# Both parts of a split operand as one moving operand of 512 columns, into two halves of a PSUM bank

## The chip, the core and the metric

The kernel runs on one core of a Trainium2 chip. Time is device time in microseconds from the first to the last instruction of one execution; smaller is better. Runs of the kernel before gave 2663.76, 2665.52 and 2670.75 us, median 2665.52 us.

## The reference

A trunk of two layers on 256 tokens of 2048 channels, all in float32: layer 0 mixes with an RWKV-7 time mix, layer 1 with a causal convolution module, and each is followed by a gated MLP (ConvGLU). Cut to what matters here:

```
F = 5504
h = modulate(rms_norm(x, g), shift, scale)            # shift, scale, gate from c: c_act @ ada_w[i]
# layer 0
r, k, v = einsum('nbtc,ncd->nbtd', x_rkv, w_rkv)      # three 2048 x 2048 linears
y = wkv7_scan(r, decay, k, v, -kk, kk * a)            # a recurrence over the 256 tokens, per head
out = ((group_norm(y) + bonus) * g) @ w_o
# layer 1
u = glu(h @ w_pw1 + b_pw1); u = causal_depthwise_conv(u, w_dw, b_dw)
out = silu(layer_norm(u)) @ w_pw2 + b_pw2
# after each
x = x + gate * out
g, val = split(h @ w_up)                              # 2048 x 11008
x = x + gate2 * ((silu(conv3(g)) * val) @ w_down)     # 5504 x 2048
```

## The kernel before

Activations lie with channels on the 128 partitions and the 256 tokens along the free axis (`T = 256`), so a linear of 2048 inputs is 16 output tiles, each a sum over 16 input tiles. Products are made in a cheap one-pass float32 form (fp32r), and to keep precision every operand is split in two: `hi` is the rounded value and `lo` the rest. Of weights, ScalarE makes `hi` (L231) and VectorE, or for some tiles GpSimd, makes `lo` (L232) in `split_w`, from a 1 MB tile `raw` that a DMA brought; `hi` and `lo` have three buffers each. Of activations, a tile `x` (`slot(F32R)`, 2 parts of 260 columns) holds part 0 (rounded) and part 1 (rest).

`mm_pair` adds one input tile's product to a PSUM accumulator with three matmuls: hi·part 0 (L237), hi·part 1 (L238), lo·part 0 (L239). Each loads its 128x128 weights anew, so `hi` is loaded twice. The linears that feed `w_up` and `w_pw1` call it with 258 columns (two columns carry the adaLN shift); all others with 256. Of the calls with 256 columns, 1376 are in the down projections (`w_dn`: 2 layers x 16 output tiles x 43 input tiles), 96 in the last six tiles of k, 256 in r (`r_tile`), 128 in half of v (`v_gen`), 40 in the first half of five `w_o` tiles during the scan (`wo_gen`), 216 in the rest of `w_o`, 208 in `w_pw2`: 2320 together. `k_outer` holds the first three `w_pw2` tiles (48 more triples) and takes its operands one at a time.

In the order of time the stages are: the first ten tiles of k beside the token mix; the last six of k; r with decay, a, and the scan's operands; the other half of v in plain fp32 (`linear_native`, L300) while VectorE inverts 32x32 blocks (`inv_step`, two interleaved chains, one for each half X[0], X[1] of a tile `raw`); the scan, in which TensorE's order is written out by hand (a heap of generators with due times); `w_o`; the ConvGLU of layer 0 in three parts of 15, 14 and 14 hidden tiles, each an up stage and a down stage; the convolution; `w_pw2`; the ConvGLU of layer 1; the final norm. The adaLN products c·ada_w ("gates", `ada`, L208) are background work: a 1 MB tile `raw`, two multiply-and-sum pieces on VectorE. They run beside the stages up to and with `w_pw2`, and a few beside the first up stage of layer 1. Outside hand-ordered places a scheduler sets the order of each engine's instructions when the program is built; each engine then runs its own in that order.

A finished accumulator is read once: by a copy on ScalarE (k, v), by a multiplication on VectorE (r, L459), by a bias on ScalarE (`w_pw2`, L1119), or by one multiply-add on VectorE into the residual (`stt`, L159: `w_o` L893, `wo_gen` L835, `w_dn` L943). The accumulators take turns over the eight PSUM banks.

Of the kernel before, what the change touches and what calls it, by code (L numbers as in the profile page):

```python
# [18 lines left out]
P = 128  # L19
T = 256  # L20
# [91 lines left out]
def trunk_kernel(ctx: ExitStack, tc: tile.TileContext, a, out):  # L112
# [42 lines left out]
    def vmul(o, x, y):  # L155
        nc.vector.tensor_tensor(out=o, in0=x, in1=y, op=ALU.mult)  # L156
# [6 lines left out]

    # ---- constants, parameters
    cst = cp.tile([P, NCC], F32, name="cst")
# [56 lines left out]

    # ---- linear layers
    def split_w(r, k0, k1, step=1024, eng=None):
# [10 lines left out]
    def mm_pair(acc, hi, lo, j, x, first, last, n=T):  # L235
        c = slice(j * P, (j + 1) * P)
        nc.tensor.matmul(acc[:, :n], lhsT=hi[:, c], rhs=x[:, 0, :n], start=first, stop=False)  # L237
        nc.tensor.matmul(acc[:, :n], lhsT=hi[:, c], rhs=x[:, 1, :n], start=False, stop=False)  # L238
        nc.tensor.matmul(acc[:, :n], lhsT=lo[:, c], rhs=x[:, 0, :n], start=False, stop=last)  # L239
# [24 lines left out]
    class k_outer:  # L264
        """some outputs together, the operands fed one at a time; the weights split ahead, two operands' at once"""

# [20 lines left out]
        def feed(self, o):  # L287
            k = self.n
            self.n += 1
            hi, lo = self.sp[k // 2]  # L290
            for w, q in ((hi, 0), (lo, 0), (hi, 1)):
                for j, acc in enumerate(self.accs):
                    c = slice((2 * j + k % 2) * P, (2 * j + k % 2 + 1) * P)
                    nc.tensor.matmul(acc[:, :T], lhsT=w[:, c], rhs=o[:, q, :T], start=k == 0 and w is hi and q == 0, stop=k == KT - 1 and q == 1)

    def linear_native(r, hs32, tag=None):
# [4 lines left out]
        return acc  # L301

    def split_x(src, o):
        nc.scalar.copy(o[:, 0, :T], src)
        vsub(o[:, 1, :T], src, o[:, 0, :T])

    # ---- rms norm
    def sq_acc(st, x):
# [15 lines left out]

    # ================= layer 0: time mix =================
    hs = [slot() for _ in range(KT // 2)]
# [30 lines left out]
    def ada_s(f):  # L357
        lw = slot().rearrange("p a t -> p (a t)")[:, :448]
        nc.sync.dma_start(out=lw, in_=a["lw1"][f])
        # scale and shift of tile f  # L360
        pa = ps("y")
        for q in range(2):
            r = raw_tile()
            nc.sync.dma_start(out=r, in_=a["ada_s"][f, q])
            for k in range(8):
                g, kk = k % 4, 8 * q + k
                nc.tensor.matmul(pa[32 * g:32 * g + 32, :T], lhsT=cc[:, kk, :], rhs=r[:, k * T:(k + 1) * T],  # L367
                                 start=kk < 4, stop=kk >= 12, skip_group_check=True)
        rk = load_w(a["w_k"][f])
        sb = t1()  # L370
        nc.scalar.copy(sb, pa[:, :T])
        for j in range(2):
            nc.tensor.matmul(pa[:, 256 + j:257 + j], lhsT=sb[:, j * P:(j + 1) * P], rhs=K("e4"), start=True, stop=True, skip_group_check=True)
        for j in range(2):
            piece = 1 - j
            vadd(mod(0, piece, f), pa[:, 256 + j:257 + j], pc("ada_b", piece * KT + f))
        stt(geff[0][:, f:f + 1], mod(0, 1, f), 1.0, pc("gam_mix", f), ALU.add, ALU.mult)
        ahead[f] = (lw, rk)
# [57 lines left out]

    # ---- k, decay, a; A, B, K of the scan; N
    for f in range(KM, KT):
        acc = linear(a["w_rkv"][1, f], xk, ("mm", "y")[f % 2])
        kt.append(t1())  # L440
        nc.scalar.copy(kt[f], acc[:, :T])
        bg(BG_K)
# [13 lines left out]
    def r_tile(f):  # L456
        r_load(f)
        acc = linears(None, xr, ("c", "y")[f % 2], T, None, [rw.pop(f)])[0]
        vmul(pv(f)[:, :, 1:L + 1], ch(acc[:, :T]), pv(f)[:, :, 1:L + 1])  # L459
        nc.sync.dma_start(out=dAR[f, :, :, 1, :], in_=pv(f)[:, :, 1:L + 1])  # L460
# [104 lines left out]

    # ---- inverse of the 32-blocks, all heads and chunks on partitions
    X = raw_tile()
# [65 lines left out]

    # ---- v, scan, group norm, bonus, gate
    def small(tag, w, bufs):
# [7 lines left out]
    def v_gen(f):  # L643
        acc = ps("mm")
        r = load_w(a["w_rkv"][2, f])
        yield 0
        for k0 in range(0, KT, 8):
            hi, lo = split_w(r, k0, k0 + 8, 512, VE[0])
            for k in range(k0, k0 + 8):
                mm_pair(acc, hi, lo, k - k0, xv[k], k == 0, k == KT - 1)  # L650
                yield VS
        vt[f] = t1()
        nc.scalar.copy(vt[f], acc[:, :T])

# [17 lines left out]
    def prep_gen(f):  # L672
# [7 lines left out]
        yield 0  # L680
        # products of A, R with B, K, and B, K by tokens
        for c in range(NC_):
# [12 lines left out]
            yield PU  # L695
        # off-diagonal block of the inverse
        py = ps("g")
# [5 lines left out]
        for h in range(2):  # L703
            r1 = slice(h * L + 32, h * L + 64)
            nc.scalar.copy(ysb[r1].rearrange("p c t -> p (c t)"), py[r1, :P])
        # bonus
        rk = t1()
# [6 lines left out]
        yield PU  # L714
        # centred V by tokens, in the other half of the partitions
        pvt = ps("g")
# [107 lines left out]

    # half of the output projection and residual, while the scan goes on
    def wo_gen(m):
        x_load(m)
        r = load_w(a["w_o"][m][:, :C // 2])
        yield 0
        acc = ps("mm")  # L830
        hi, lo = split_w(r, 0, KT // 2, 512, VE[0])
        for k in range(KT // 2):
            mm_pair(acc, hi, lo, k, yo[k], k == 0, k == KT // 2 - 1)
            yield VS
        stt(xview(m), acc[:, :T], mod(0, 2, m), xview(m))  # L835

# [24 lines left out]
    with tc.manual_schedule(engines={mybir.EngineType.PE}):  # L861
        while heap:
# [4 lines left out]
            if d is not None:  # L867
                at(t + d, g)
    # ---- output projection and residual
    # gain * x, with the shift in the last columns: the products of the two are rstd-free  # L870
    def operand(l, which, f):
# [16 lines left out]
    for f in range(KT):  # L888
        x_load(f)
        if f >= max(NG, NWO):  # L890
            ada(0, 2, f)
        acc = waccs[f] if f < 3 else w_o(f)
        stt(xview(f), acc[:, :T], mod(0, 2, f), xview(f))  # L893
        ops.append(operand(0, 1, f))
        sq_acc(st, xview(f))
# [5 lines left out]

    # ---- ConvGLU
    def ffn(l, st, ops, nops):
# [14 lines left out]
        for f0, f1 in PARTS:  # L918
# [22 lines left out]
            for f in range(KT):  # L941
                acc = linear(a["w_dn"][l, f][:, f0 * P:f1 * P], hid, None, T, half(f, DNP))
                stt(xview(f), acc[:, :T], mod(l, 5, f), xview(f))  # L943
                if f1 == FT:
# [13 lines left out]

    # ================= layer 1: conformer convolution =================
    ops = nops  # L960
# [23 lines left out]

    # n of the taps on the tensor engine, m on GpSimd, the others on the vector engine in two chains
    def tap(f, d):
# [127 lines left out]
    for f in range(KT):  # L1114
# [3 lines left out]
        t = t1()  # L1118
        act(t, acc[:, :T], bias=pc("b_pw2", f))  # L1119
        stt(xview(f), t, mod(1, 2, f), xview(f))  # L1120
# [4 lines left out]

    # ---- final norm
    rstd = rstd_of(st)
# [108 lines left out]
```

## Time and profile before

| | |
|---|---|
| three runs | 2663.76, 2665.52, 2670.75 us; median 2665.52 |
| profiled execution, span | 2670.5 us; its own time is not given apart from the span |
| mean granted TensorE clock | 0.977 of full |
| TensorE matmul / weight load busy | 2520.7 us (94%) / 2404.8 us (90%) |
| VectorE / ScalarE / GpSimd busy | 2003.9 us (75%) / 1357.1 us (51%) / 464.0 us (17%) |
| HBM | 614.30 MB read, 235 GB/s over the span |

A matmul's end in the profile is modelled (it is pipelined), so "busy" says that TensorE had work, not how fast it ran; the distance from one matmul's start to the next one's says that. It is read from a stretch without gaps as length divided by count.

### The profile page before, as it was taken

To read this page: it belongs to the slowest core of one execution; us is meant where nothing else is said; L and a number is where in the kernel's file an instruction comes from. 1 tells how busy PE (TensorE), PEld (TensorE's weight loads), DVE (VectorE), ACT (ScalarE), POOL (GpSimd) and SP (SyncE) were. 2 spreads that over 40 slices of the span, in tenths; PEclk is the share of its full clock that TensorE was granted. 3 is DMA by queue.
4 is the path that set the end of the run, shared out by engine and by line. 5 is a ranking of instruction groups with operands and counts; after the bars stand their busy time and mean duration, and the time that the engine had idled before them with its cause. 6 is when DMAs were issued, how large, how long until landed. Compare 5 with 4: busy or idle time off the path is not lost.

```text
span 2670.5 us, 52899 instructions
## 1 busy us (share of the span) xinstructions
PE 2520.7 (94%) x21250; PEld 2404.8 (90%) x21250; DVE 2003.9 (75%) x3635; ACT 1357.1 (51%) x2650; POOL 464.0 (17%) x452
## 2 busy tenths in 40 slices
PE   6899996999999999999999999978899999999998
PEld 3678885877799999999999999967899999999997
DVE  4567767768688888887878979979988656656665
ACT  4565622556555543553455555554555445534553
POOL 0000015544000012001100248954200000000000
PEclk9999997989999999999999999989999999999999
DMA  8887766677277778777978844436777655555553
GB/s 312 316 312 268 211 207 209 230 218 240 78 284 278 283 285 331 292 281 290 336 263 296 305 161 164 168 127 243 286 275 273 220 188 188 170 190 190 178 175 126
DMA packets 154805, 630.84 MB, mean 236 GB/s; under 512 B 60480, under 2 KB 72256, under 8 KB 95936
## 3 DMA queue, kind: packets, MB, share of 16 engines
q1 hardware_dynamic: 153824, 624.85, 65.9%
q8 instruction: 166, 2.72, 0.4%
q0 software_dynamic: 736, 2.62, 0.3%
q14 instruction: 79, 0.65, 0.1%
HBM read 614.30 MB, written 13.11 MB: 235 GB/s over the span
## 4 chain that ended last, share of the span: by engine, by line
PE 76%; DVE 10%; DMA 7%; ACT 3%; issue 2%; POOL 1%; SPq 0%; DVEq 0%; POOLq 0%; ACTq 0%
PE ps L237 22%; PE ps L239 22%; PE ps L238 21%; DMA raw<-ada 4%; DVE raw L208 3%; DVE s L159 2%; DVE lo L232 1%; PE ps L367 1%; PE ps L300 1%; DMA raw<-ada_s 1%; POOL lo L232 1%; DVE s L156 1%; PE ps L687 1%; ACT hi L231 1%; PE ps L398 1%
## 5 line engine op out<-in xcount | busy, mean ns | idle before, releaser
L237 PE MATMUL ps<-s,hi 128*128 128x258 f32 (+1 forms) x5584 | 1594.8, 286 | 7.5 <-ACT hi L231 6.4
L239 PE MATMUL ps<-s,lo 128*128 128x258 f32 (+1 forms) x5584 | 1581.6, 284 | 20.8 <-DVE lo L232 18.9
L238 PE MATMUL ps<-s,hi 128*128 128x258 f32 (+1 forms) x5584 | 1579.8, 283 | 0.6 <-DVE s L153 0.6
L231 ACT CAST hi<-raw 128x1024 fp32r<-128x1024 f32 (+6 forms) x873 | 769.7, 897 | 881.8 <-PE ps L238 606.1
L239 PEld LDWEIGHTS ps<-s,lo 128*128 128x128 f32 x5584 | 1063.7, 191 | 29.4 <-DVE lo L232 22.8
L237 PEld LDWEIGHTS ps<-s,hi 128*128 128x128 f32 x5584 | 1060.2, 190 | 16.8 <-ACT hi L231 8.6
L238 PEld LDWEIGHTS ps<-s,hi 128*128 128x128 f32 x5584 | 1063.4, 190 | 4.5 <-issue 3.0
L232 DVE TENSOR_TENSOR lo<-raw,hi 128x1024 fp32r<-128x1024 f32 (+4 forms) x639 | 746.0, 1171 | 303.5 <-ACT hi L231 301.8
L232 POOL TENSOR_TENSOR lo<-raw,hi 128x512 fp32r<-128x512 f32 x234 | 335.2, 1458 | 957.5 <-ACT hi L231 623.4
L208 DVE CUSTOM_DVE_ANT_0 raw<-raw,cb,par 128x1024 f32<-128x1024 f32 x156 | 213.2, 1367 | 76.0 <-DMA raw<-ada 71.3
L208 DVE CUSTOM_DVE_ANT_0 raw<-raw,cb,md 128x1024 f32<-128x1024 f32 x156 | 214.9, 1378 | 0.9
L159 DVE SCALAR_TENSOR_TENSOR s<-ps,par,s 128x239 f32<-128x239 f32 (+26 forms) x420 | 166.0, 456 | 1.8 <-ACT s L162 1.2
L1135 POOL TENSOR_TENSOR s<-s,t 128x256 f32<-128x256 f32 x6 | 4.1, 727 | 751.4 <-DVE t L322 751.4
L156 DVE TENSOR_TENSOR t<-ps,t 128x256 f32<-128x256 f32 x188 | 79.2, 422 | 47.5 <-PE ps L239 43.8
L159 DVE SCALAR_TENSOR_TENSOR s<-ps,md,s 128x256 f32<-128x256 f32 x117 | 55.9, 480 | 41.8 <-PE ps L239 41.7
L159 DVE SCALAR_TENSOR_TENSOR t<-t,par,t 128x255 f32<-128x255 f32 (+1 forms) x172 | 82.6, 480 | 1.9 <-ACT t L162 0.6
L156 DVE TENSOR_TENSOR s<-ps,cst 64x64 f32<-64x64 f32 (+2 forms) x208 | 48.1, 253 | 37.7 <-ACT n L689 27.0
L162 ACT ACTIVATE t<-t,par 128x256 f32<-128x256 f32 x118 | 68.1, 587 | 5.6 <-DVE t L156 2.5
L162 ACT ACTIVATE t<-t 128x256 f32<-128x256 f32 x102 | 42.5, 417 | 37.9 <-DVE t L159 24.1
L687 PE MATMUL ps<-s,s 128*128 128x128 f32 x256 | 46.6, 308 | 11.6 <-ACT s L694 10.6
L300 PE MATMUL ps<-s,raw 128*128 128x256 f32 x256 | 56.0, 380 | 0.0
L300 PEld LDWEIGHTS ps<-s,raw 128*128 128x128 f32 x256 | 48.4, 190 | 6.9 <-issue 0.3
(199 smaller groups left out, 2167.2 us busy)
## 6 DMA issues: line engine op xcount, KB each, us to landing
raw<-w_up SPq DMA_DIRECT2D x172, 1024.0 KB, 4.9
raw<-ada SPq DMA_DIRECT2D x156, 1024.0 KB, 6.7
raw<-w_dn SPq DMA_DIRECT2D x64, 896.0 KB, 4.7
raw<-w_pw SPq DMA_DIRECT2D x48, 1024.0 KB, 4.9
raw<-w_rkv SPq DMA_DIRECT2D x38, 1024.0 KB, 6.0
raw<-ada_s SPq DMA_DIRECT2D x32, 1024.0 KB, 6.4
raw<-w_dn SPq DMA_DIRECT2D x32, 960.0 KB, 4.9
raw<-w_o SPq DMA_DIRECT2D x11, 1024.0 KB, 4.9
```

The lines of the kernel that those rows point to most:

```text
L156: nc.vector.tensor_tensor(out=o, in0=x, in1=y, op=ALU.mult)
L159: nc.vector.scalar_tensor_tensor(out=o, in0=x, scalar=s, in1=y, op0=op0, op1=op1)
L162: nc.scalar.activation(out=o, in_=i, func=func, bias=bias, scale=scale)
L208: nc.vector.tensor_tensor_reduce(out=r[q], in0=r[q], in1=cb[:, q * w:(q + 1) * w], scale=1.0, scalar=mod(l, piece, f) if q else pc("ada_b" ...
L231: nc.scalar.copy(hi[:, s], v[:, s])
L232: (eng or nc.vector).tensor_tensor(out=lo[:, s], in0=v[:, s], in1=hi[:, s], op=ALU.subtract)
L237: nc.tensor.matmul(acc[:, :n], lhsT=hi[:, c], rhs=x[:, 0, :n], start=first, stop=False)
L238: nc.tensor.matmul(acc[:, :n], lhsT=hi[:, c], rhs=x[:, 1, :n], start=False, stop=False)
L239: nc.tensor.matmul(acc[:, :n], lhsT=lo[:, c], rhs=x[:, 0, :n], start=False, stop=last)
L300: nc.tensor.matmul(acc[:, :T], lhsT=r[:, k * P:(k + 1) * P], rhs=hs32[k], start=k == 0, stop=k == n - 1)
L367: nc.tensor.matmul(pa[32 * g:32 * g + 32, :T], lhsT=cc[:, kk, :], rhs=r[:, k * T:(k + 1) * T], start=kk < 4, stop=kk >= 12, skip_group_che ...
L687: nc.tensor.matmul(pg[:, h * P:(h + 1) * P], lhsT=bkc, rhs=ari[h][:, c].rearrange("p j t -> p (j t)"), start=True, stop=True, skip_group_c ...
```

## The change

Where the operand has 256 columns, hi·part 0 and hi·part 1 become one matmul: both parts are one moving operand of 2 x 256 columns, and the result goes into the two halves of the bank (first half hi·part 0, second half hi·part 1). lo·part 0 is added to the second half. Each of the 2368 triples (2320 and the 48 of `k_outer`) becomes two matmuls with two weight loads, with as many columns in all (512 + 256). The sum of the halves is made when the accumulator is read: `both` copies one half on ScalarE and adds the other on VectorE; `both_res` makes two multiply-adds into the residual where there was one. r's product moves from VectorE to GpSimd behind such a sum. The linears of 258 columns stay as they are.

```diff
     def mm_pair(acc, hi, lo, j, x, first, last, n=T):
         c = slice(j * P, (j + 1) * P)
+        if n == T:
+
+            nc.tensor.matmul(acc.rearrange("p (a t) -> p a t", a=2), lhsT=hi[:, c], rhs=x[:, :, :T], start=first, stop=False, skip_group_check=True)
+            nc.tensor.matmul(acc[:, T:], lhsT=lo[:, c], rhs=x[:, 0, :T], start=False, stop=last, skip_group_check=True)
+            return
         nc.tensor.matmul(acc[:, :n], lhsT=hi[:, c], rhs=x[:, 0, :n], start=first, stop=False)
...
-            for w, q in ((hi, 0), (lo, 0), (hi, 1)):
-                for j, acc in enumerate(self.accs):
-                    c = slice((2 * j + k % 2) * P, (2 * j + k % 2 + 1) * P)
-                    nc.tensor.matmul(acc[:, :T], lhsT=w[:, c], rhs=o[:, q, :T], start=k == 0 and w is hi and q == 0, stop=k == KT - 1 and q == 1)
+            for j, acc in enumerate(self.accs):
+                mm_pair(acc, hi, lo, 2 * j + k % 2, o, k == 0, k == KT - 1)
...
+    def both(o, acc):
+        nc.scalar.copy(o, acc[:, T:])
+        vadd(o, acc[:, :T], o)
+
+    def both_res(x, acc, s):
+        stt(x, acc[:, :T], s, x)
+        stt(x, acc[:, T:], s, x)
...
-        nc.scalar.copy(kt[f], acc[:, :T])
+        both(kt[f], acc)
...
-        vmul(pv(f)[:, :, 1:L + 1], ch(acc[:, :T]), pv(f)[:, :, 1:L + 1])
+        rt = t1()
+        both(rt, acc)
+        nc.gpsimd.tensor_tensor(out=pv(f)[:, :, 1:L + 1], in0=ch(rt), in1=pv(f)[:, :, 1:L + 1], op=ALU.mult)
...
-        nc.scalar.copy(vt[f], acc[:, :T])
+        both(vt[f], acc)
...
-        stt(xview(m), acc[:, :T], mod(0, 2, m), xview(m))
+        both_res(xview(m), acc, mod(0, 2, m))
...
-                stt(xview(f), acc[:, :T], mod(l, 5, f), xview(f))
+                both_res(xview(f), acc, mod(l, 5, f))
...
-        act(t, acc[:, :T], bias=pc("b_pw2", f))
+        act(t, acc[:, T:], bias=pc("b_pw2", f))
+        vadd(t, acc[:, :T], t)
```

In the built program VectorE gets 163 instructions (117 `stt` from PSUM and 46 additions from PSUM) and loses 16 (r's products), ScalarE gets 16 copies, GpSimd 16 products.

TensorE, last down stage of layer 1, before (`s` are the activations' tiles, `ps` the accumulator):

```order
L237 MATMUL ps_30605<-s_30145,hi_30634 128x256
L238 MATMUL ps_30605<-s_30145,hi_30634 128x256
L239 MATMUL ps_30605<-s_30145,lo_30635 128x256
L237 MATMUL ps_30662<-s_28377,hi_30663 128x256
L238 MATMUL ps_30662<-s_28377,hi_30663 128x256
L239 MATMUL ps_30662<-s_28377,lo_30664 128x256
```

and in the changed kernel, where the lines of `mm_pair` are L239 and L240:

```order
L239 MATMUL ps_28404<-s_27092,hi_28405 128x512
L240 MATMUL ps_28404<-s_27092,lo_28406 128x256
L239 MATMUL ps_28404<-s_27228,hi_28405 128x512
L240 MATMUL ps_28404<-s_27228,lo_28406 128x256
L239 MATMUL ps_28404<-s_27364,hi_28405 128x512
L240 MATMUL ps_28404<-s_27364,lo_28406 128x256
```

Three rows for each input tile have become two, the first of them with 512 columns.

VectorE, first down stage of layer 0, before (`L232` makes a weight's `lo`, `L208` is a gate, and the row with `ps` and `md` adds a finished accumulator to the residual):

```order
L159 SCALAR_TENSOR_TENSOR s_8326<-ps_11510,md_72,s_8326 128x256
L232 TENSOR_TENSOR lo_11637<-raw_11633,hi_11636 128x1024
L232 TENSOR_TENSOR lo_11665<-raw_11633,hi_11664 128x896
L208 ISA raw_11749,md_73<-raw_11749,cb,par 128x1024
L208 ISA md_73 128x1
L159 SCALAR_TENSOR_TENSOR s_8326<-ps_11572,md_72,s_8326 128x256
L232 TENSOR_TENSOR lo_11694<-raw_11690,hi_11693 128x1024
```

and in the changed kernel:

```order
L232 TENSOR_TENSOR lo_11082<-raw_11058,hi_11081 128x896
L208 ISA raw_11101,md_73<-raw_11101,cb,md_73 128x1024
L208 ISA md_73 128x1
L159 SCALAR_TENSOR_TENSOR s_8039<-ps_11010,md_72,s_8039 128x256
L232 TENSOR_TENSOR lo_11109<-raw_11105,hi_11108 128x1024
L159 SCALAR_TENSOR_TENSOR s_8039<-ps_11010,md_72,s_8039 128x256
L159 SCALAR_TENSOR_TENSOR s_8147<-ps_11060,md_72,s_8147 128x256 x2
```

Each accumulator now takes two additions, in VectorE's own order between the `lo` pieces that TensorE needs next.

VectorE at the end of the inverse, before; the rows with `raw_3963` are its steps (`s_3967` belongs to the second chain), `L208` is a gate, and the last row is the inverse's last step:

```order
L627 MEMSET raw_3963 128x32
L150 TENSOR_TENSOR raw_3963<-raw_3963,s_3967 128x28x3
L208 ISA raw_4367,md_72<-raw_4367,cb,par 128x1024
L208 ISA md_72 128x1
L156 TENSOR_TENSOR s_3967<-raw_3963 128x58
L208 ISA raw_4367,md_72<-raw_4367,cb,md_72 128x1024
L208 ISA md_72 128x1
L150 TENSOR_TENSOR raw_3963<-raw_3963,s_3967 128x29x2
L156 TENSOR_TENSOR s_3967<-raw_3963 128x30
L208 ISA raw_4512,md_72<-raw_4512,cb,par 128x1024
L208 ISA md_72 128x1
L150 TENSOR_TENSOR raw_3963<-raw_3963,s_3967 128x30
```

and in the changed kernel, a stretch that begins 48 rows ahead of the inverse's last step (`s_3668` is the first chain's scratch, `s_3669` the second's; `ps_4073` with `cst` are masked products of the scan's first tile):

```order
L208 ISA raw_4199,md_72<-raw_4199,cb,par 128x1024
L208 ISA md_72 128x1
L156 TENSOR_TENSOR s_3668<-raw_3665 128x84
L641 MEMSET raw_3665 128x32
L150 TENSOR_TENSOR raw_3665<-raw_3665,s_3669 128x21x10
L156 TENSOR_TENSOR s_3674<-ps_4073,cst 64x64
L156 TENSOR_TENSOR s_3675<-ps_4073,cst 64x64
L208 ISA raw_4199,md_72<-raw_4199,cb,md_72 128x1024
L208 ISA md_72 128x1
L150 TENSOR_TENSOR raw_3665<-raw_3665,s_3668 128x28x3
L645 COPY s_4040<-raw_3665 128x512
L156 TENSOR_TENSOR s_3669<-raw_3665 128x198
```

Before, three gate pieces and no masked product stand ahead of the inverse's last step (counted from the inverse's beginning); now six gate pieces and twelve masked products (four chunks of three) do.

## Rows read from the trace of the kernel before

**Rows 1.** The page's first and fourth parts: busy time of each engine, and the chain.
```profile
PE 2520.7 (94%) x21250; PEld 2404.8 (90%) x21250; DVE 2003.9 (75%) x3635; ACT 1357.1 (51%) x2650; POOL 464.0 (17%) x452
...
PE 76%; DVE 10%; DMA 7%; ACT 3%; issue 2%; POOL 1%; SPq 0%; DVEq 0%; POOLq 0%; ACTq 0%
```

**Rows 2.** Windows by stage: stretch, length; busy (x) PE, PEld, DVE, ACT, POOL; clock, DMA, GB/s.
```profile
184.00:225.00 41.00, 40.94 (x330) 39.97 (x330) 31.02 (x39) 23.04 (x42) 0.14 (x2) 1.00 0.88 326
225.00:357.00 132.00, 130.32 (x1082) 112.53 (x1082) 100.37 (x184) 79.51 (x126) 12.54 (x35) 1.00 0.72 218
357.00:437.00 80.00, 66.09 (x352) 58.56 (x352) 54.64 (x173) 15.77 (x44) 27.86 (x23) 0.93 0.61 198
437.00:720.00 283.00, 255.70 (x2802) 215.15 (x2802) 199.36 (x508) 162.27 (x564) 113.46 (x114) 0.92 0.62 203
720.00:799.00 79.00, 77.15 (x623) 75.48 (x624) 63.43 (x111) 42.31 (x78) 0.00 (x0) 0.98 0.67 243
971.00:1058.00 87.00, 85.80 (x722) 85.39 (x721) 74.17 (x97) 33.43 (x43) 25.82 (x16) 1.00 0.83 314
1218.00:1304.00 86.00, 82.01 (x678) 81.39 (x676) 68.25 (x97) 31.49 (x43) 20.39 (x16) 0.98 0.85 318
1465.00:1549.00 84.00, 80.95 (x676) 79.78 (x675) 76.87 (x131) 44.46 (x92) 21.74 (x18) 1.00 0.83 299
1822.00:1911.00 89.00, 73.65 (x560) 71.37 (x560) 89.00 (x131) 41.32 (x89) 39.20 (x24) 0.94 0.71 270
2089.00:2174.00 85.00, 85.00 (x722) 85.00 (x721) 45.43 (x51) 32.50 (x36) 0.00 (x0) 1.00 0.56 191
2174.00:2336.00 162.00, 162.00 (x1345) 162.00 (x1344) 103.20 (x139) 83.87 (x139) 0.00 (x0) 1.00 0.52 180
2336.00:2415.00 79.00, 79.00 (x671) 79.00 (x670) 42.83 (x50) 30.47 (x34) 0.00 (x0) 1.00 0.57 192
2577.00:2657.00 80.00, 79.56 (x676) 79.35 (x674) 46.10 (x63) 36.55 (x53) 0.00 (x0) 1.00 0.42 139
```

**Rows 3.** Groups by line and shape, TensorE: one of three lines of `mm_pair`, 256 columns.
```profile
L239 PE MATMUL ps<-s,lo 128*128 128x256 f32 x2320 | 658.7, 285 | 20.0 <-DVE lo L232 18.1 <-POOL lo L232 1.9
```

**Rows 4.** Groups of the page: the plain fp32 matmuls (L300) and their weight loads.
```profile
L300 PE MATMUL ps<-s,raw 128*128 128x256 f32 x256 | 56.0, 380 | 0.0
...
L300 PEld LDWEIGHTS ps<-s,raw 128*128 128x128 f32 x256 | 48.4, 190 | 6.9 <-issue 0.3
```

**Rows 5.** Timeline of TensorE: start, length of a merged run, count.
```profile
365.65 6.64 PE L300 MATMUL ps<-s,raw 128*128 128x256 f32 x30
```

**Rows 6.** Timeline of weight loads: eight loads that feed matmuls of one column.
```profile
1645.34 0.98 PEld L982 LDWEIGHTS ps<-cst,s 128*128 128x128 f32 x8
```

**Rows 7.** Groups of the page, VectorE: pieces that read PSUM, and one gate.
```profile
L156 DVE TENSOR_TENSOR t<-ps,t 128x256 f32<-128x256 f32 x188 | 79.2, 422 | 47.5 <-PE ps L239 43.8
...
L159 DVE SCALAR_TENSOR_TENSOR s<-ps,md,s 128x256 f32<-128x256 f32 x117 | 55.9, 480 | 41.8 <-PE ps L239 41.7
...
L208 DVE CUSTOM_DVE_ANT_0 raw<-raw,cb,par 128x1024 f32<-128x1024 f32 x156 | 213.2, 1367 | 76.0 <-DMA raw<-ada 71.3
```

**Rows 8.** Waits of VectorE, first down stage of layer 0.
```profile
DVE raw L208 <- DMA raw<-ada: 9.2, 6, 3.2
```

**Rows 9.** Groups on VectorE in the `w_pw2` stage: the longest of one shape.
```profile
L159 DVE SCALAR_TENSOR_TENSOR s<-t,md,s 128x256 f32<-128x256 f32 x13 | 11.3, 870 | 0.0
```

**Rows 10.** Timeline of VectorE: first and last step of the inverse, masked products.
```profile
380.01 0.19 DVE L156 TENSOR_TENSOR s<-raw 128x30 f32<-128x30 f32 x1 [15.65 <-DMA raw<-dN]
...
428.41 0.20 DVE L150 TENSOR_TENSOR raw<-raw,s 128x30 f32<-128x30 f32 x1
...
428.65 0.66 DVE L156 TENSOR_TENSOR s<-ps,cst 64x64 f32<-64x64 f32 x3
```

**Rows 11.** Waits of TensorE in the scan stage.
```profile
PE ps L702 <- DMA tn<-dTn: 4.5, 1, 4.5
...
PE ps L730 <- DMA s<-dT: 4.2, 1, 4.2
```

More of the change, by code (lines that the diff above doesn't have):

```diff
@@ L892, in trunk_kernel @@
         acc = waccs[f] if f < 3 else w_o(f)
-        stt(xview(f), acc[:, :T], mod(0, 2, f), xview(f))
+        both_res(xview(f), acc, mod(0, 2, f))
         ops.append(operand(0, 1, f))
```

## Prediction

> **What bounds the kernel now.** I read the page first: TensorE has work for 94% of the span and makes up 76% of the chain that ended last, VectorE 10% of it [rows 1]. That average hides stages with different limits, so I cut the span into stages [rows 2] and compared TensorE's length per matmul with VectorE's busy time. In the two down stages of layer 1 without a gap, 85.00 us hold 722 matmuls and 79.00 us hold 671: 117.7 ns from start to start, at a granted clock of 1.00 (2.4 GHz), with VectorE busy little over half. There nothing but the matmul's own beat counts. In layer 0 the down stages carry the gates as well: VectorE is busy 74.17 of 87, 68.25 of 86 and 76.87 of 84 us, and DMA moves 299 to 318 GB/s. The `w_pw2` stage is the other extreme: VectorE is busy for all of its 89.00 us, TensorE for 73.65. The scan and what leads to it wait on chains of short pieces.
>
> **What a triple costs, and a pair.** Of the matmuls with 256 columns there are 2320 on each of three lines [rows 3]; three of them take 3 x 117.7 = 353.1 ns. The trace has no fp32r matmul of 512 columns, so its beat x is bounded. From above: columns alone set the beat, and 512 take twice what 256 take, x = 235.4; the gain g = 353.1 - (x + 117.7) is then nothing. From below: at 2.4 GHz and a column a cycle 512 columns need 213.3 ns, so 256 need 106.7, and 11.0 ns of each 117.7 are something else. What that is decides. Eight weight loads that feed matmuls of one column, where no stream of columns can be the limit, take 0.98 us [rows 6]; less 0.19 for the last one's own length, the mean of such a load [rows 4], that is 0.79 / 7 = 113 ns a load. A load is therefore longer than 106.7 ns of columns, and a triple looks like three loads in a row, each not quite hidden. The plain fp32 matmul has a longer beat, (6.64 - 0.38) / 29 = 215.9 ns [rows 4, 5], and its load costs nothing visible. I take x = 215.9 as the nearest row: a long matmul covers the load behind it, g = 353.1 - 215.9 - 117.7 = 19.5 ns. At most the short matmul too falls to the 113 ns of the load, g = 24.
>
> The Trainium skill (TensorE: Matmul & The Clock Gate, "Back-to-back issue gap") gives the gap as N / 2.4 + 2.5 ns, 109.2 for 256 columns and 215.8 for 512. By it alone a triple is 327.5 and a pair 325.0, and the change is worth 2.5 ns a triple. The trace disagrees for 256 columns (117.7) and agrees for the longer plain matmul. The same page ("LDWEIGHTS (loading the stationary operand)") gives a load of 128 columns 107 ns, which with the 113 ns above speaks for the load as what is left.
>
> **The change, part by part** (gain with g = 19.5, against the profiled span):
> - Layer 1's down stages: 688 triples, all on the path. VectorE gets 16 more pieces of 480 ns [rows 7], 7.7 us, beside 45.43 of 85 and 42.83 of 79 us [rows 2]: hidden. -13.4 us.
> - `w_o`: 216 triples are 4.2 us. VectorE goes from 63.43 of 79 us to 71.1 of 75 and will be late now and then. I take -3.
> - k: 96 triples, 1.9 us, but the stage moves 326 GB/s, the most of any [rows 2]. -1.5. r: 256 triples, 5.0 us, TensorE at 130.32 of 132 us. VectorE trades a product for an addition, GpSimd's 16 products lie beside 12.54 busy of 132 us. -4.
> - v and `wo_gen` in the scan: 168 triples, 3.3 us. TensorE has 27 us without work there, so part of the gain becomes wait. Half: -1.5.
> - Layer 0's down stages: again 688 triples or 13.4 us, but VectorE gets 7.7 us a stage. Busy plus new is 81.9, 76.0 and 84.6 of 87, 86 and 84; the third is already over. Its idle 37.7 us in the three stages (87 - 74.17 and so on) is largely waits for a gate's DMA, 9.2 us in the first [rows 8], which shrink if VectorE comes later. If the cover holds the sum is -13.4, if the waits stay as they are it is +23. Queued behind a late addition are the `lo` pieces that TensorE waits for (18.1 us over the kernel, [rows 3]). I take -2.
> - `w_pw2`: 16 more additions from PSUM on the engine that has no idle time: 16 x 0.422 [rows 7] = +6.7 us. TensorE's 4.1 us for 208 triples buy nothing. Bounds: nothing if they fill a hole, 13.9 if they were stretched as the SBUF form of this stage, 870 ns [rows 9], where the same operation from PSUM has 480 over all stages. `k_outer` now waits for an operand's rest before its first matmul; its 0.9 us go there: 0.
> - The end of the inverse. In the new order three more gate pieces (1.37 us each, [rows 7]) and four groups of masked products (0.66 us, [rows 10]) stand ahead of the inverse's last step, which releases the copy that the scan waits for: TensorE stood 4.5 and 4.2 us for it [rows 11]. 3 x 1.37 + 4 x 0.66 = 6.7 us; the gates are then done and don't come later. The products also wait for TensorE. Bounds 0 and 10; I take +4.
>
> Sum: -13.4 - 3 - 1.5 - 4 - 1.5 - 2 + 6.7 + 4 = -14.7 us. The profiled span is 2670.5 us, 5.0 over the median of the three runs and within them, so I subtract from the median: 2665.5 - 14.7 = **2651 us**.
>
> **Rivals.**
> *Columns set the beat.* x = 235.4, g = 0: a matmul's reading of its operand takes 0.46 ns a column whatever the load does. For it: 258 columns take 162.00 / 1345 = 120.4 ns [rows 2], 2.7 ns more for two columns, which a load that is the limit would not show. Against it: the plain matmul's 215.9, and the bare load's 113. All TensorE terms vanish, the costs stay: +6.7, +4, and in layer 0's down stages about a quarter of the 23 us that VectorE gets, +6: 2682 us, slower. It decides from g below about 9 ns on: the TensorE terms are worth 1.2 us per ns (23.4 / 19.5), so 9 ns just pay the 10.7 us of `w_pw2` and the inverse. The Trainium skill's gap formula gives 2.5 ns, which is this case with 3 us less.
> *A fixed price per matmul.* The 11.0 ns belong to each matmul, whatever its length: x = 224.3, g = 11.1. 13.3 us of gain against 10.7 of cost and about 1 in layer 0: 2664 us, no change.
> *VectorE takes TensorE's place in layer 0.* g is as forecast, but the gates' waits do not shrink and every added piece delays a `lo`: the three stages cost 23 us instead of gaining 2. For it: 84.6 of 84 us in the third. Against it: gates are background work and 37.7 us idle are there. It decides once more than some 15 of the 23 us are not covered: -14.7 + 2 + 23 = +10, 2676 us; with half of them covered 2664.
>
> **Chances and numbers.** Forecast 0.50 (its own range 2640 to 2660: g from 15 to 24 and the bounds of `w_pw2` and the inverse), fixed price 0.18, columns 0.17, VectorE 0.15. Three runs of this kernel spread by 0.26%, so 0.3%, 8 us, is about what tells a change from none. Faster: 0.46 of the forecast and 0.04 of the others; slower: 0.14 of the columns and 0.06 of VectorE; the rest, 0.30, no change. The range 2640 to 2680 reaches from the best of the forecast to the columns' case and leaves out about a tenth on either side.
>
> **What would show it.** In layer 1's down stages a pair should take 334 ns from one 512-column start to the next, and a stage of 240 pairs about 80 us in place of 85; 353 ns would be the columns, 342 the fixed price. `w_pw2` should be some 7 us longer with VectorE busy throughout. In layer 0 the down stages should stay near 86 us with VectorE above 90%. From the start of the inverse's first step to its last, VectorE should need some 7 us more than the 48.6 from 380.01 to 428.61 before [rows 10]. The prediction fails if x is not near 216, or if the new order starts the scan much later than I allow.

## The result, and the profile after

The changed kernel is slower. Its runs gave 2687.72 to 2698.05 us, median 2690.31; runs of the kernel before beside them 2663.76 to 2683.42, median 2669.91. The ratio is 1.0081 with a 95% interval of 1.0056 to 1.0107: 15 to 29 us more. The forecast was 2651 us with a range up to 2680.

The page of the changed kernel, first and fourth parts, in the form of [rows 1]:

```profile
PE 2517.1 (94%) x18882; PEld 2284.5 (85%) x18882; DVE 2065.2 (77%) x3782; ACT 1359.9 (51%) x2665; POOL 476.7 (18%) x468
...
PE 76%; DVE 11%; DMA 6%; issue 2%; ACT 2%; POOL 1%; SPq 1%; DVEq 0%; ACTq 0%; POOLq 0%
```

TensorE issues 2368 matmuls fewer and its weight loads lose 120 us, yet it is busy as long as before. The two forms of `mm_pair` (groups by line and shape; to [rows 3]):

```profile
L239 PE MATMUL ps<-s,hi 128*128 128x512 f32 x2368 | 865.5, 406 | 14.2 <-DVE s L1118 8.1 <-DVE s L159 2.6 <-ACT hi L231 2.5
L240 PE MATMUL ps<-s,lo 128*128 128x256 f32 x2368 | 670.8, 285 | 21.9 <-DVE lo L232 20.5 <-POOL lo L232 1.1
```

Windows by stage, columns as in [rows 2]:

```profile
225.00:358.00 133.00, 128.78 (x815) 98.48 (x815) 99.53 (x177) 80.29 (x135) 19.39 (x42) 0.99 0.68 214
358.00:457.00 99.00, 68.32 (x362) 58.66 (x360) 67.94 (x191) 18.01 (x50) 34.68 (x32) 0.87 0.63 210
457.00:737.00 280.00, 254.72 (x2635) 202.00 (x2636) 195.65 (x513) 160.87 (x563) 108.24 (x112) 0.93 0.59 190
990.00:1075.00 85.00, 84.40 (x479) 73.23 (x477) 78.13 (x112) 33.30 (x43) 25.65 (x16) 1.00 0.84 317
1840.00:1935.00 95.00, 79.46 (x403) 66.94 (x404) 93.83 (x146) 41.65 (x86) 41.77 (x24) 0.91 0.73 274
2111.00:2195.00 84.00, 84.00 (x481) 73.42 (x480) 51.58 (x65) 32.63 (x35) 0.00 (x0) 1.00 0.56 195
2356.00:2434.00 78.00, 78.00 (x449) 68.24 (x448) 49.12 (x65) 30.73 (x34) 0.00 (x0) 1.00 0.57 196
```

In the two down stages of layer 1 without a gap a pair takes 2 x 84.00 / 481 = 349 and 2 x 78.00 / 449 = 347 ns, where a triple took 353: about 5 ns gained, not 19.5. The row that stands out is 358 to 457: 99 us in place of the 80 from 357 to 437. To add up the whole I took landmarks from both traces, each counted from the first matmul of k's last six tiles (184.1 us before, 184.4 after). The scan's first use of `tn` comes at 254.1 before and 272.5 after, +18.4; the scan's last product is 16.5 late, layer 0's end 17.6, layer 1's first down matmul 22.3 (the stage of `w_pw2` is 4.7 longer), and layer 1 gives 4.7 back. The loss is made ahead of the scan and carried to the end.

How it is made shows in two timelines. TensorE, changed kernel; L303 are v's plain fp32 matmuls (two records each), L508 the 64x64 products that N, the inverse's input, is made from:

```profile
358.04 5.34 PE L303 MATMUL ps<-s,raw 128*128 128x256 f32 x24
363.31 0.68 PE L508 MATMUL ps<-s,s 64*64 64x64 f32 x16
...
364.54 5.88 PE L303 MATMUL ps<-s,raw 128*128 128x256 f32 x26
370.35 1.15 PE L508 MATMUL ps<-s,s 64*64 64x64 f32 x32
```

Before, one plain matmul stood ahead of the first of these N groups in place of twelve:

```profile
355.17 0.59 PE L300 MATMUL ps<-s,raw 128*128 128x256 f32 x2
355.69 0.68 PE L494 MATMUL ps<-s,s 64*64 64x64 f32 x16
...
356.93 5.88 PE L300 MATMUL ps<-s,raw 128*128 128x256 f32 x26
362.74 1.15 PE L494 MATMUL ps<-s,s 64*64 64x64 f32 x32
```

The last N group starts 7.6 us later: 2.9 because the plain matmuls themselves start later (358.04 against 355.17), 4.7 by the eleven that were put ahead. So N's DMA lands later and so does everything behind it. VectorE, changed kernel, from the inverse's first step to its last (to [rows 10]); the `COPY` row is the second of the two copies of the inverse's first half, from which the scan's `tn` is loaded:

```profile
387.71 0.19 DVE L156 TENSOR_TENSOR s<-raw 128x30 f32<-128x30 f32 x1 [15.73 <-DMA raw<-dN]
...
418.13 2.28 DVE L208 CUSTOM_DVE_ANT_0 raw<-raw,cb,par 128x1024 f32<-128x1024 f32 x1
...
429.15 1.28 DVE L208 CUSTOM_DVE_ANT_0 raw<-raw,cb,par 128x1024 f32<-128x1024 f32 x1 [2.87 <-DMA raw<-ada]
...
439.75 0.58 DVE L645 COPY s<-raw 128x512 f32<-128x512 f32 x1
...
447.87 0.21 DVE L150 TENSOR_TENSOR raw<-raw,s 128x30 f32<-128x30 f32 x1
```

It starts 7.7 us later than before and takes 60.4 us in place of 48.6: gate pieces stand in it, one of them waits 2.87 us for its own DMA with the inverse queued behind, and some pieces run far longer than usual while GpSimd works (its rows stand in the last section). The same copy before:

```profile
421.59 0.58 DVE L631 COPY s<-raw 128x512 f32<-128x512 f32 x1
```

Before, no gate piece and no masked product ran between the inverse's first step and this copy; in the changed kernel four gate pieces and six masked products do, and the stretch takes 52.0 us in place of 41.6. TensorE waits there twice, for the scan's first products (L687 before, L701 now) and for `tn` (4.5 us before, [rows 11]). The first wait before, and both in the changed kernel:

```profile
PE ps L687 <- ACT s L694: 8.7, 1, 8.7
```

```profile
PE ps L701 <- ACT s L708: 16.5, 1, 16.5
PE ps L716 <- DMA tn<-dTn: 12.1, 1, 12.1
```

### The profile page after: what moved, and what is told of

It is laid out like the page before. It is cut to its first block, busy times and chain, and to the rows that moved or that the text cites. A ratio compares the mean times of both kernels' runs of the same rounds, so it can differ in the third digit from the quotient of the medians.

```text
span 2688.4 us, 48358 instructions
## 1 busy us (share of the span) xinstructions
PE 2517.1 (94%) x18882; PEld 2284.5 (85%) x18882; DVE 2065.2 (77%) x3782; ACT 1359.9 (51%) x2665; POOL 476.7 (18%) x468
## 4 chain that ended last, share of the span: by engine, by line
PE 76%; DVE 11%; DMA 6%; issue 2%; ACT 2%; POOL 1%; SPq 1%; DVEq 0%; ACTq 0%; POOLq 0%
PE ps L242 14%; PE ps L239 14%; PE ps L243 14%; PE ps L244 14%; PE ps L240 7%; DVE raw L208 4%; DMA raw<-ada 3%; DVE s L159 2%; DVE lo L232 2%; PE ps L303 2%; DMA raw<-ada_s 1%; PE ps L379 1%; DVE s L156 1%; POOL lo L232 1%; PE ps L701 1%
## 5 line engine op out<-in xcount | busy, mean ns | idle before, releaser
L232 DVE TENSOR_TENSOR lo<-raw,hi 128x1024 fp32r<-128x1024 f32 (+4 forms) x639 | 748.9, 1174 | 297.2 <-ACT hi L231 295.4
L242 PE MATMUL ps<-s,hi 128*128 128x258 f32 x3264 | 928.0, 285 | 2.2 <-ACT hi L231 2.1
L243 PE MATMUL ps<-s,hi 128*128 128x258 f32 x3264 | 924.0, 283 | 0.1
L244 PE MATMUL ps<-s,lo 128*128 128x258 f32 x3264 | 919.9, 282 | 2.4 <-DVE lo L232 2.3
L239 PE MATMUL ps<-s,hi 128*128 128x512 f32 x2368 | 865.5, 406 | 14.2 <-DVE s L1118 8.1
L240 PE MATMUL ps<-s,lo 128*128 128x256 f32 x2368 | 670.8, 285 | 21.9 <-DVE lo L232 20.5
L244 PEld LDWEIGHTS ps<-s,lo 128*128 128x128 f32 x3264 | 621.6, 191 | 3.3 <-DVE lo L232 3.2
L243 PEld LDWEIGHTS ps<-s,hi 128*128 128x128 f32 x3264 | 620.3, 190 | 0.8 <-DVE s L159 0.3
L242 PEld LDWEIGHTS ps<-s,hi 128*128 128x128 f32 x3264 | 617.3, 189 | 3.8 <-ACT hi L231 2.9
L239 PEld LDWEIGHTS ps<-s,hi 128*128 128x128 f32 x2368 | 451.6, 191 | 125.4 <-issue 12.0
L232 POOL TENSOR_TENSOR lo<-raw,hi 128x512 fp32r<-128x512 f32 x234 | 336.0, 1460 | 957.5 <-ACT hi L231 738.3
L240 PEld LDWEIGHTS ps<-s,lo 128*128 128x128 f32 x2368 | 455.8, 192 | 33.4 <-DVE lo L232 26.9
L208 DVE CUSTOM_DVE_ANT_0 raw<-raw,cb,par 128x1024 f32<-128x1024 f32 x156 | 214.9, 1377 | 48.0 <-DMA raw<-ada 47.0
L208 DVE CUSTOM_DVE_ANT_0 raw<-raw,cb,md 128x1024 f32<-128x1024 f32 x156 | 212.5, 1362 | 0.9
L159 DVE SCALAR_TENSOR_TENSOR s<-ps,md,s 128x256 f32<-128x256 f32 x234 | 110.8, 480 | 30.6 <-PE ps L240 28.4
```

The lines of the kernel that those rows point to most:

```text
L159: nc.vector.scalar_tensor_tensor(out=o, in0=x, scalar=s, in1=y, op0=op0, op1=op1)
L208: nc.vector.tensor_tensor_reduce(out=r[q], in0=r[q], in1=cb[:, q * w:(q + 1) * w], scale=1.0, scalar=mod(l, piece, f) if q else pc("ada_b" ...
L232: (eng or nc.vector).tensor_tensor(out=lo[:, s], in0=v[:, s], in1=hi[:, s], op=ALU.subtract)
L239: nc.tensor.matmul(acc.rearrange("p (a t) -> p a t", a=2), lhsT=hi[:, c], rhs=x[:, :, :T], start=first, stop=False, skip_group_check=True)
L240: nc.tensor.matmul(acc[:, T:], lhsT=lo[:, c], rhs=x[:, 0, :T], start=False, stop=last, skip_group_check=True)
```

## The experiments

Ratios are to runs of the kernel before on the same chip, with a 95% interval. Runs of one kernel spread over some 20 us and each has one profile, so a stage length that only one profile shows is taken as a hint. The scan shows how far: it took 278.8, 274.8 and 288.8 us in the profiles of three kernels with the same scan (before, `e9`, `e10`). Three profiles are of runs far from their kernel's median: `e5` 2687.6 us (median 2671.8), `e10` 2680.6 (2673.3), `e6` 2680.8 (2691.3).

**What sets the beat** (`e1_beats`). In outline:

```python
for i in range(64):   # one such stretch for each form; a new weight slice each time
    nc.tensor.matmul(acc[:, :n], lhsT=w[:, slice_i], rhs=x[:, :n], start=i == 0, stop=i == 63)
```

> This kernel leaves the whole computation out: it only runs stretches of 64 matmuls back to back, one form a stretch, and is read by the start-to-start time of each. Columns theory (what the trace of the changed kernel suggests): an fp32r matmul costs about 0.455 ns a column of its moving operand whatever the weight load does, so 128 columns about 60 (or the load's 113 where that is longer), 256 about 117, 384 about 175, 512 about 233 ns, the two segments with a gap the same as 512 in one piece, and with weights of only 32 columns still 117 and 233. Load theory (the prediction's): with weights of 32 columns the 256-column matmul falls towards 107 to 110, and 512 columns towards 216. Segment theory: 512 columns in one piece take 216, only the two segments of 256 in two halves of a bank take 233. bf16 operands of 256 and 512 columns show whether the four-byte type pays: by the type theory they take 107 to 110 and 213 to 216, by the other theories the same as fp32r.

Timeline of TensorE, one row a stretch (start, length of the merged run, count):

```profile
28.45 7.26 PE L147 MATMUL acc<-x,w 128*128 128x128 f32 x64
35.54 7.69 PE L149 MATMUL acc<-x,w 128*128 128x256 f32 x64
43.06 11.25 PE L151 MATMUL acc<-x,w 128*128 128x384 f32 x64
54.15 15.00 PE L153 MATMUL acc<-x,w 128*128 128x512 f32 x64
68.99 7.66 PE L155 MATMUL acc<-x,w 128*32 128x256 f32 x64
76.49 15.08 PE L157 MATMUL acc<-x,w 128*32 128x512 f32 x64
91.41 7.16 PE L159 MATMUL acc<-xb,wb 128*128 128x256 bf16 x64
98.40 13.98 PE L165 MATMUL acc<-xb,wb 128*128 128x512 bf16 x62
112.22 27.79 PE L167 MATMUL acc<-rx,raw 128*128 128x256 f32 x128
```

The length less that of the last matmul itself (0.27 to 0.40 us), over 63: fp32r takes 111, 117.6, 173 and 232 ns for 128, 256, 384 and 512 columns. From 256 columns on that is 0.45 to 0.46 ns a column. With weights of 32 columns, whose loads take 108 ns of the engine's time in place of 188, the two sizes still take 117 and 233: the load is not the limit. L153 is the two-segment operand of the change; the stretch of 512 in one piece ran first, its matmuls at first 427 ns apart, although the granted clock of those windows reads 1.00, and then 231 to 237. bf16 takes 109 and, counting the two records that are missing, 13.6 / 63 = 216. The plain fp32 stretch has 128 records for its 64 matmuls, 216 ns each. So the columns theory holds, and the price belongs to the fp32r type. The 215.9 ns that I had taken as the nearest row is one half of a plain fp32 matmul over 256 columns; it says nothing of a stream of 512.

**Which part loses** (`e2_without_k_r`, `e3_only_k_r`, `e4_r_product_vector`). A flag on `mm_pair` lets single linears keep the three matmuls and the one reading piece:

```diff
-        if n == T:
+        if n == T and wide:
...
-        acc = linear(a["w_rkv"][1, f], xk, ("mm", "y")[f % 2])
+        acc = linear(a["w_rkv"][1, f], xk, ("mm", "y")[f % 2], wide=False)
```

> All of the change but k's and r's linears, so that the order ahead of the scan is that of the kernel before. Order theory (the later scan start, from the new order around r's linears and the inverse, is all of the loss): the inverse's first and last steps, the first use of tn and the chain's last product come within 2 us of the kernel before, and the time is that of the kernel before within 5 us: -2 in layer 1's down stages, +3 to +5 in w_pw2. Rival (the wide form costs everywhere, by VectorE's additions from PSUM in layer 0's down stages, w_o and w_pw2): at least 12 us over the kernel before.

> Only k's and r's linears in the wide form, all else as before; the order ahead of the scan is that of the changed kernel (six gates, twelve groups of masked products and 25 of the 32-column matmuls' native rivals ahead of the same points). Order theory: 15 to 20 us over the kernel before, the scan's start 17 to 19 us late, nothing else moved. Rival: under 5 us.

> The changed kernel with r's product on VectorE as before, in place of GpSimd: the addition and the product then both run on VectorE. Order theory: the order of the gates and masked products against the inverse stays as in the changed kernel, so the loss stays: 14 to 22 us over the kernel before. Rival (GpSimd's slower product delays the row state and so the last N matmul and the inverse): most of the loss goes, under 8 us over the kernel before.

Measured: 1.0049 (1.0031 to 1.0067), 1.0095 (1.0069 to 1.0120) and 1.0124 (1.0102 to 1.0146). k and r alone make a loss as large as the whole change, and GpSimd's product is not its cause. But what is left without them costs 8 to 18 us too, against what I expected, although its scan starts as early as before (table below). The two parts do not add up: 13 and 25 us against 20. `e4`, 27 to 39 us, also lies over what I expected; nothing here says why.

**TensorE's order** (`e5_late_native`, `e7_before_late_native`). On the changed kernel, and on the kernel before:

```diff
-        acc = linear_native(vraw.pop(f) if f in vraw else load_w(a["w_rkv"][2, f]), xv32, ("c", "y")[f % 2])
+        with tc.issue_after(nl[0].ins):     # nl[0]: the last N matmul
+            acc = linear_native(vraw.pop(f) if f in vraw else load_w(a["w_rkv"][2, f]), xv32, ("c", "y")[f % 2])
```

> The changed kernel, with v's plain matmuls queued behind the last N matmul on TensorE and nothing else changed. That alone takes the six gate pieces and the masked products out of the inverse in VectorE's order too. Order theory: the inverse's first step comes 7 us earlier than in the changed kernel, the inverse takes about 49 us in place of 60, and the scan starts 15 to 20 us earlier: 12 to 20 us less than the changed kernel, so 0 to 8 us over the kernel before. Rival (the additions of r's and k's linears are late themselves, whatever the order): less than 5 us regained.

> The kernel before, with the same queueing of v's plain matmuls behind the last N matmul, no wide linear. Order theory: 14 of the plain matmuls and three gate pieces leave the stretch ahead of the inverse's end, the scan starts 4 to 9 us earlier, and the time is 3 to 9 us under the kernel before. Rival (TensorE then stands idle for the N matmul and the plain matmuls come later): no gain, or a loss of up to 6 us.

Measured: 1.0010 (0.9992 to 1.0028) and 0.9973 (0.9954 to 0.9992). The first takes back all but about 3 of the changed kernel's 20 us with every wide linear in place; the second beats the kernel before. Timeline of VectorE in `e7_before_late_native`, first and last step of the inverse: 38 us, with no gate in it.

```profile
372.54 0.19 DVE L156 TENSOR_TENSOR s<-raw 128x30 f32<-128x30 f32 x1 [12.48 <-DMA raw<-dN]
...
410.61 0.21 DVE L150 TENSOR_TENSOR raw<-raw,s 128x30 f32<-128x30 f32 x1
```

**The order alone** (`e13_before_early_native`, `e14_early_native_gates_behind`) **and VectorE's part of it** (`e6_gates_behind_inverse`). The kernel before, with no wide linear, gets the changed kernel's order of twelve and thirteen plain matmuls ahead of the N groups; VectorE's order then follows by itself. In the second and third, on the same kernel and on the changed one, the scan's VectorE work is queued behind two instructions: `xl`, the second copy of the inverse's first half, and `xm`, which sets the diagonal of its second half. That is not the end of the inverse, as the expectations have it: by the traces no gate and no masked product is left ahead of the copy, but four gate pieces and twelve masked products still run ahead of the last step, in both:

```diff
+            if len(nv) in (12, 25):             # nv: v's plain matmuls so far
+                for m in nl[13 if len(nv) == 12 else 14]:      # N's matmuls by tile
+                    tc.add_manual_dep(m.ins, nv[-1].ins.name, ...)   # order only
...
-    with tc.manual_schedule(engines={mybir.EngineType.PE}):
+    with tc.issue_after(xl.ins), tc.issue_after(xm.ins), tc.manual_schedule(engines={mybir.EngineType.PE}):
```

> The kernel before, no wide linear at all, with the one order of the changed kernel put in by hand on TensorE: twelve of v's plain matmuls ahead of the N matmuls of one tile and thirteen ahead of those of the last two (before: one and thirteen). VectorE's order then follows, six gate pieces and twelve masked products ahead of the inverse's end, as in the changed kernel. Order theory: the scan starts 15 to 19 us later than before, and the time is 14 to 22 us more than before. Rival (the order costs only together with the wide linears' own additions): under 8 us.

> The same, with the scan's gates and masked products queued behind the end of the inverse on VectorE. If VectorE's order inside the inverse is what the delay turns into a loss, most of it is regained and the time is 3 to 8 us over before. If, as between the changed kernel and its own variant of this kind, the gates only move the loss into the scan, it stays within 5 us of the run without this.

> The changed kernel, with the scan's work on VectorE (its gates and its masked products) queued behind the end of the inverse, and TensorE's order left as it is, so that the last N matmul still stands behind 25 plain matmuls. If VectorE's order inside the inverse costs what its steps lost (11.8 us) and TensorE's order the 7 us before it, the inverse starts as late as in the changed kernel and takes 49 us: 8 to 13 us less than the changed kernel. If the gates only move the loss (they come later, in the scan, where VectorE is short): under 4 us regained.

Measured: 1.0092 (1.0068 to 1.0116), 1.0022 (1.0008 to 1.0037) and 1.0071 (1.0046 to 1.0095). The order by itself costs 18 to 31 us, as much as the changed kernel loses; the scan of `e13` starts 22.5 us late, more than expected. TensorE in `e13_before_early_native`, whose rows repeat those of the changed kernel, and its waits:

```profile
358.06 5.34 PE L300 MATMUL ps<-s,raw 128*128 128x256 f32 x24
...
364.57 5.88 PE L300 MATMUL ps<-s,raw 128*128 128x256 f32 x26
370.38 1.15 PE L497 MATMUL ps<-s,s 64*64 64x64 f32 x32
```

```profile
PE ps L691 <- ACT s L698: 15.2, 1, 15.2
PE ps L706 <- DMA tn<-dTn: 15.0, 1, 15.0
```

With the gates behind the copy most of this comes back in the kernel before, although TensorE's order stays, but in the changed one nothing that the interval shows. Landmarks from the traces, us from the first matmul of k's last six tiles:

| kernel | last N matmul | inverse, first step | second copy | last step | `tn` first used | ratio |
|---|---|---|---|---|---|---|
| before | 179.6 | 195.9 | 237.5 | 244.3 | 254.1 | 1 |
| changed | 186.9 | 203.3 | 255.3 | 263.4 | 272.5 | 1.0081 |
| `e2` without k, r | 179.3 | 195.2 | 237.1 | 243.8 | 253.2 | 1.0049 |
| `e3` only k, r | 186.2 | 202.4 | 254.5 | 262.6 | 271.6 | 1.0095 |
| `e5` changed, plain matmuls late | 183.1 | 197.6 | 233.5 | 235.3 | 249.9 | 1.0010 |
| `e6` changed, gates behind | 187.5 | 203.7 | 243.3 | 259.3 | 257.0 | 1.0071 |
| `e7` before, plain matmuls late | 176.3 | 189.6 | 225.8 | 227.7 | 250.4 | 0.9973 |
| `e13` before, plain matmuls early | 188.4 | 205.0 | 256.2 | 264.6 | 276.6 | 1.0092 |
| `e14` the same, gates behind | 185.1 | 201.9 | 240.5 | 255.6 | 255.3 | 1.0022 |

(`tn` comes from the first of the inverse's two halves, which in `e6` and `e14` is done well ahead of the second.) In `e6` the scan starts only 2.9 us later than before, and then takes 286.8 us from the first `tn` to the last product, against 276.9 in the changed kernel and 280.5 in `e14`. The gates may move the loss there into a scan whose VectorE also has the wide linears' additions, but 286.8 lies within the spread of an unchanged scan (274.8 to 288.8), so that is not shown, and why `e6` regains nothing in time stays open.

**What is left** (`e8_without_k_r_pw2`, `e9_only_down1`, `e10_only_down0`, `e12_late_native_no_pw2`, `e11_down1_late_native`). The edits are the same flag on other linears, and in the last two the queueing of `e5`.

> All of the change but k, r and w_pw2: v, w_o and both layers' down linears are wide. If w_pw2 is the cost that is left without k and r, the stage from the conv's broadcast to layer 1's first down matmul takes the 302 us of the kernel before, and the time is within 3 us of it. Rival (layer 0's down stages and the scan pay as well): 5 us or more over the kernel before.

> Only layer 1's down linears wide, where TensorE alone is the path. Columns theory: a pair takes about 350 ns where a triple took 353, so 688 of them gain 2 to 3 us, not to be told from no change. The prediction's step (334 ns, 13.4 us): a ratio of 0.995.

> Only layer 0's down linears wide. The prediction's step: 2 us less than before. VectorE theory (with nothing gained on TensorE, each stage's 7.7 us of added pieces on VectorE is covered only in part): 4 to 10 us more than before. If the waits for the gates cover all of it: within 2 us of before.

> The changed kernel with v's plain matmuls queued behind the last N matmul and without w_pw2's part: the two named costs are taken out. The changed kernel with the queueing alone was at 1.0010; w_pw2 cost 0.0034 between two other kernels. If both costs add, 0.997 to 0.999, 3 to 8 us less than before; if w_pw2's cost is hidden by something else here, 1.001 again.

> The kernel before with v's plain matmuls queued behind the last N matmul, and layer 1's down linears wide: the two things that gained. The queueing alone had 0.9973 of the kernel before; with 2 to 3 us of the down linears 0.996 to 0.997, 8 to 11 us less than before. If the down linears give nothing, 0.997 again.

Measured, in this order: 1.0015 (0.9999 to 1.0031), 1.0005 (0.9988 to 1.0022), 1.0023 (1.0005 to 1.0040), 1.0007 (0.9990 to 1.0024) and 0.9979 (0.9960 to 0.9998). `w_pw2`: from the convolution's broadcast of its mean to layer 1's first down matmul the ten profiles of this study with a plain `w_pw2` show 300.8 to 301.9 us, the five with a wide one 306.0 to 308.1, about 5 us. In time, leaving it out gave 0.0034 between `e2` and `e8`, and 0.0003 between `e5` and `e12`; each difference is uncertain by some 0.0025, so both agree with 5 us and the second with nothing as well. `e12` came out on the second of its two expectations, and the time alone does not show what `w_pw2` costs; `e8`, at 4 us, lies between its two. Layer 1's down linears alone give nothing that can be measured. Windows of `e9_only_down1`, in its two stages without a gap:

```profile
2080.00:2163.00 83.00, 83.00 (x477) 72.51 (x476) 51.35 (x64) 31.83 (x35) 0.00 (x0) 1.00 0.56 193
2326.00:2404.00 78.00, 78.00 (x445) 67.85 (x444) 48.90 (x64) 30.15 (x34) 0.00 (x0) 1.00 0.57 194
```

They hold 348 and 351 ns a pair, and the three stages with the up stages between them are 1.7 us shorter than before, as the columns theory has it. Layer 0's down linears alone cost 1 to 11 us in time, but the part of their profile from layer 0's MLP to its end is as long as before (746.9 against 747.0), and what that profile has over the kernel before lies in its scan, which the change does not touch: where the loss sits stays open. `e11` is faster than both kernels, with an interval that ends just under 1; its median gives no reason to prefer it to `e7`.

## Why the prediction was wrong

*Step that failed first: "I take x = 215.9 as the nearest row: a long matmul covers the load behind it, g = 353.1 - 215.9 - 117.7 = 19.5 ns."* x is 232 ns, and g about 4. All TensorE terms hang on it: at 1.2 us per ns they were 18.6 us too large. With g = 4 the sum would have been +4 us, 2669, no change. Of the evidence, the bare load of 113 ns was right (128 columns take 111, no less), but a load that nearly fills 117.7 ns need not set it. The rival's own argument decided it beforehand: two columns more cost 2.7 ns, which a load that is the limit would not show, and I gave that 0.17. The Trainium skill (TensorE: Matmul & The Clock Gate, "Back-to-back issue gap") has a formula for an isolated matmul, by which 256 and 512 columns are estimated at 109.2 and 215.8 ns; the bf16 stretches agree (109 and 216) and the fp32r ones do not (117.6 and 232). That the plain matmul of the trace agreed with the 215.8 was no evidence: its record is of 256 columns.

*Second: "The end of the inverse [...] Bounds 0 and 10; I take +4."* It was +18.4. I counted what the new order put ahead of the inverse's last step on VectorE, 6.7 us, and it was 11.8: the counted pieces cost about what I took, the rest is waiting and longer steps. But what the scan needs first of the inverse is not its last step, as the term has it: it is `tn`, whose second copy is made earlier, and from the first step to that copy VectorE needs 10.5 us more, which is over the bound by itself. And I did not look at what the new order does ahead of the inverse's first step on TensorE, eleven more plain matmuls of 0.43 us in front of N's products; with the plain matmuls' own later start (2.5 us from k's first matmul) the inverse starts 7.3 us late. `e13` shows that this one order makes the whole loss without a wide linear, `e14` that most of it goes through VectorE's order ahead of the copy (2 to 10 us are left of 18 to 31; on the changed kernel, `e6`, the same edit gave nothing back in time), and `e5` that the wide linears without it lose about 3 us.

The two account for 18.6 and 14.4 of the 39 us between forecast and result; the kernel before itself ran 4.4 us slower beside the result than in the runs that I started from.

The other terms, from single profiles where nothing else is said:
- Layer 1's down stages, -13.4: the stages from the first of them to the end are 4.7 us shorter in the changed kernel, 1.7 in `e9`; of the 4.7, 2.4 lie in the two up stages between them, which the change leaves as they are.
- `w_pw2`, +6.7: about 5, and VectorE busy 93.83 of 95 us. Right.
- k and r, -5.5: v's plain matmuls start 2.5 us later, not earlier. GpSimd's product was as harmless as I took it.
- Layer 0's down stages, -2, with VectorE above 90%: the three stages are 2.7 us shorter, VectorE busy for 92 to 95% of them. Right in size in this profile; the time of `e10` speaks for a small loss instead.
- `w_o` (-3) and the scan (-1.5): within the spread of single profiles, no gain can be read.

Of the rivals, *Columns set the beat* named the mechanism (350 ns a pair, forecast 353) and the sign, and its 2682 us lacks the order's cost and has 6 us for layer 0 that the profile of the changed kernel does not show. *VectorE takes TensorE's place in layer 0* and *a fixed price per matmul* are not what happened: 342 ns a pair was not reached.

What stays open: why the scheduler put the plain matmuls ahead, why the costs of `e2` and `e3` do not add up, where `e10` loses, and why `e6` regains nothing.

## What to carry to other kernels

Before counting on a longer matmul, measure its beat by itself in the same data type: where a stretch without gaps already runs at the price of its columns, merging matmuls saves weight loads that nobody waits for. When a change moves a scheduler's order, read every engine's order ahead of the one transfer that a stage waits for, from that transfer back to its first producer, not only the engine on which pieces were added. An order that came out badly can be set by hand, and here setting it was worth more than the change: 7 us (2 to 12) on the kernel before.

## What was not expected of the hardware

- One fp32r column costs 0.45 to 0.46 ns from 256 columns on, a bf16 column 0.42 (216 / 512), both at a granted clock of 1.00; two segments with a gap cost nothing extra (232 ns, and 233 for one piece with short weights).
- VectorE and GpSimd seem to hold each other up, now one and now the other. GpSimd's pieces of `lo` in the changed kernel (its lengths are rough in the profile):

```profile
409.16 10.17 POOL L232 TENSOR_TENSOR lo<-raw,hi 128x512 fp32r<-128x512 f32 x1 [29.83 <-ACT hi L231]
...
434.24 5.30 POOL L232 TENSOR_TENSOR lo<-raw,hi 128x512 fp32r<-128x512 f32 x4
```

  and steps of the inverse on VectorE in these stretches, the last one with GpSimd at rest:

```profile
415.17 0.63 DVE L150 TENSOR_TENSOR raw<-raw,s 128x238 f32<-128x238 f32 x2
...
434.36 1.28 DVE L150 TENSOR_TENSOR raw<-raw,s 128x58 f32<-128x58 f32 x1
...
447.37 0.22 DVE L150 TENSOR_TENSOR raw<-raw,s 128x58 f32<-128x58 f32 x1
```

  Up to 418.13 VectorE's steps follow each other at their usual lengths, and one piece of GpSimd's takes 10.17 us. From there on it is VectorE that is held up while GpSimd works: a gate of 1.28 us (at 429.15) takes 2.28 (at 418.13), and a step of 0.22 us takes 1.28 where four pieces of GpSimd's take 5.30. No run was made to part the two.

- In the changed kernel the up stages of layer 1, which it does not touch, take 161.1 us where the kernel before takes 162.3: 161.1 to 161.3 in all six profiles with a wide k and r, 161.8 to 162.4 in the nine others. A 258-column matmul is there some 0.9 ns shorter. No run tells why.
